# Moving preparation, gate closing, branch loads and the projection seam of a decoder-layer kernel

## The chip, the cores and the metric

The kernel runs on one core of one Trainium2 chip. The time is device microseconds of one execution, and the median over several executions is what counts.

## The reference

One layer of a hybrid decoder on 1024 tokens of width 1024, in float32. What is computed, cut to the main lines:

```python
h = rms_norm(x, norm1_g)
p_rwkv, p_sb, q_mem, gate_logits = split(h @ w_in)      # 1792, 1536, 512, 3072 columns
y_a = rwkv7_branch(p_rwkv, ...)       # 8 heads of 64: token shift, decay, delta-rule state, group norm
y_b = stick_breaking_branch(p_sb)     # 8 heads of 64, strictly causal
y_m = memory_branch(q_mem, mem, ...)  # 4 heads of 128 over 256 memory tokens
x = x + (sum_b sigmoid(gate_b) * (y_b @ w_branch[b])) @ w_out
h = rms_norm(x, norm2_g) @ w_up                          # 5632 columns
x = x + (silu(conv3(h)[gate]) * conv3(h)[value]) @ w_down
```

## The kernel before

Every matrix product is done with three matmuls on rounded operands: a number is split into a high part (an ACT copy to the type fp32r) and a low part (the difference, on DVE or POOL), and high·high, high·low and low·high are added in PSUM (`mm3`, L87). A projection of 128 columns over 1024 tokens takes eight steps of six matmuls, and the kernel treats one such step as the unit of interleaving.

The first half of the layer is written as Python generators that are woven together in `run`. A "main" stream (`rwkv_prep` for four pairs of heads, then `sb_attn`, `mem_attn`, `stage2` with the recurrent state, `group_norm`) takes a step, and a "pump" of projections (`items`: shifted projections of the recurrent branch, values, keys and queries, gates, memory projections, branch products) fills with a set number of steps for each (`weave`, L1631). The order in which an engine gets its instructions is then made by a planner that simulates the program with its own costs: it may move an instruction on its engine, except for those that are pinned (`pinned`, L108), each of which stays behind the instruction of its engine that the program gave just before it. All TensorE work from the recurrent preparation on is pinned. Most ACT, DVE and POOL work and all DMA issues are not. ACT, DVE and POOL then run their lists in order, and so does the queue of SP, which issues most loads.

Names that the change and the prediction touch:

- `shifted` (L241) takes a projection out of PSUM on DVE (L248), has ACT make the shifted copy (L249) and DVE join the two (L251). `shift_item` calls it after the eighth step.
- `rwkv_prep` has for each pair of heads two halves: `chain` makes the operands `bk` (L381) and `ra` (L382 to L384) on DVE, `decayed` (L410) scales `bk` on POOL, `gram` multiplies both on TensorE and masks the result on DVE (L398), `turned` transposes what `decayed` made. PSUM has four banks of tag `g` for these and four of tag `mm` for projections.
- `proj_item` is one projection of the pump; `gate_item` evicts one of gate logits (L739), multiplies with the row norm on DVE (L740), and leaves its sigmoid (L743) and its store (L745, on the ACT queue) to `close_gates`, which the next projection calls. The tile of the gate is one of three buffers of tag `w4`, which also serve keys, queries and squares.
- `norm_quarter` normalizes a quarter of the recurrent output in ten steps, laid between the twelve steps in which `stage2` makes the next quarter: sums, squares, the power -1/2 on POOL (`rsqrt`, L169), then four multiplications on DVE (L593).
- `load_y` loads four tiles of a branch's result (L1110) and rounds them (L1101 ACT, L1102 DVE) for `branch_item`. The loads go through `w4`; the low parts lie in four buffers of tag `A`, which the memory attention also uses; the high parts in one buffer `inst`.
- `out_proj` multiplies the merged branches with `w_out`, tile by tile of 128 tokens (`mm`). `norm` adds the residual (L1230), squares (L1231), takes the power on POOL, scales (L1235); `spread` transposes (two evictions per bank on ACT, two on DVE: L1250, L1252), `sums` (L1261 to L1266) and `split` (L1271, L1272) make the operands of the next stage.
- `up_phase` is a two-by-two block scheme of seven products instead of eight. `step(n, i)` is product i of column pair n, twelve matmuls. Its operands B11, B21, B22, T1 to T4 are what `split` makes. `hl` splits a weight (ACT L1351, POOL L1354).

Of the kernel before, what the change touches and what calls it, by code (L numbers as in the profile page):

```python
# [20 lines left out]
C = 64  # L21
# [6 lines left out]
OFF = 19.4  # L28
# [21 lines left out]
class Trunk:  # L50
# [120 lines left out]
    def startup(self):  # L171
# [41 lines left out]
        self.wa = self.shifted(12, "A", pps[0])  # L213
        nc.scalar.activation(self.wa[0:64], self.wa[0:64], AF.Tanh)
        self.sg = self.shifted(13, "A", pps[1])
        nc.scalar.activation(self.sg, self.sg, AF.Sigmoid)
        return self.shifted(4, "at", pps[2])
# [24 lines left out]
    def shifted(self, ti, tag, pp=None):  # L242
        nc = self.nc
        pp = pp or self.proj(self.I["w_in"][ti])
        pr, tmp = self.t4(), self.t4()
        nc.vector.memset(tmp[:, 0:1], 0.0)
        for h in range(2):
            nc.vector.tensor_tensor(pr[:, h * 512 : (h + 1) * 512], pp[h], self.nrb[:, h * 512 : (h + 1) * 512], ALU.mult)  # L248
        nc.scalar.activation(tmp[:, 1:1024], pr[:, 0:1023], AF.Copy, scale=self.mun[:, ti : ti + 1])  # L249
        out = self.t4(tag)  # L250
        nc.vector.scalar_tensor_tensor(out, pr, self.omm[:, ti : ti + 1], tmp, ALU.mult, ALU.add)  # L251
        return out
# [35 lines left out]
    def shift_item(self, ti, out, name):  # L288
# [10 lines left out]
        out.append(self.shifted(ti, "at", pp))  # L299
        self.fresh.append(name)  # L300
        yield
# [5 lines left out]
    def rwkv_prep(self, p, krv, need):  # L307
# [66 lines left out]
        def chain(h):  # L374
            hs = halves[h]
            bk, ra = self.t4("qk"), self.t4("qk")
            bk4, ra4 = (x.rearrange("p (c u s) -> p c u s", c=8, u=2) for x in (bk, ra))
            for x, first in ((b, 1), (kp, 0)):
# [3 lines left out]
            nc.vector.tensor_tensor(ra4[:, :, 0], self.c8(r[:, hs]), self.c8(P[:, hs]), ALU.mult)  # L382
            nc.vector.scalar_tensor_tensor(ra4[:, :, 1, 1:64], self.c8(P[:, hs])[:, :, 0:63], -1.0, self.c8(kk[:, hs])[:, :, 1:64], ALU.mult, ALU.mult)
            nc.vector.tensor_scalar(ra4[:, :, 1, 0], self.c8(kk[:, hs])[:, :, 0], -math.exp(OFF), None, ALU.mult)  # L384
# [188 lines left out]
    def norm_quarter(self, i, junk):  # L573
# [17 lines left out]
        yield  # L591
# [102 lines left out]
    def proj_item(self, src, fin, hook={}):  # L694
# [200 lines left out]
    def mem_kv(self):  # L895
# [18 lines left out]
        def ss():  # L914
            pst = self.ps("g")
            for j in range(2):
                for k in range(8):
                    o = (k % 4) * 256 + j * 128
                    self.colsum(pst[:, j : j + 1], sqs[k // 4][:, o : o + 128], self.ones[:, 0:1], k == 0, k == 7)
# [86 lines left out]
    def mem_q(self, h, out, hook):  # L1006
# [3 lines left out]
        def fin(pp):  # L1010
            sq = self.t4()
            qhi, qlo = self.t4("qk", F32R), self.t4("qk", F32R)
            for i in range(2):
                hs = slice(i * 512, (i + 1) * 512)
                nc.scalar.activation(qhi[:, hs], pp[i], AF.Copy, scale=self.par("memq"))
                nc.scalar.activation(sq[:, hs], pp[i], AF.Square)
                nc.vector.scalar_tensor_tensor(qlo[:, hs], pp[i], self.par("memq"), qhi[:, hs].bitcast(F32), ALU.mult, ALU.subtract)
# [127 lines left out]
    def branch(self, b, first):  # L1145
        st = {}

        def load():
            st["y"] = self.load_y(b)
# [6 lines left out]
        return load, items  # L1156
# [43 lines left out]
    def out_proj(self):  # L1200
# [21 lines left out]
        def norm(tt, pp):  # L1222
            x = self.t4()
# [4 lines left out]
            for n in range(2):  # L1228
                ns = slice(n * 512, (n + 1) * 512)
                nc.vector.tensor_tensor(x[:, ns], pp[n], x[:, ns], ALU.add)  # L1230
                nc.scalar.activation(sq[:, ns], x[:, ns], AF.Square, accum_out=ss[:, n : n + 1])  # L1231
            nc.scalar.dma_start(self.x2d[tt], x)
            nc.vector.tensor_tensor(rs, ss[:, 0:1], ss[:, 1:2], ALU.add)
            self.rsqrt(rs, rs, 1, 1.0 / D, 1e-6)
            nc.scalar.activation(sq, x, AF.Copy, scale=rs)  # L1235
            return sq

        def spread(tt, sq):
            tl = slice((tt % 4) * 128, (tt % 4 + 1) * 128)
            for kb in range(2):  # L1240
# [4 lines left out]
                for kk in range(4):  # L1245
# [3 lines left out]
                    if kk < 2:  # L1249
                        nc.scalar.activation(dst, src, AF.Copy, scale=self.par("g2", k))  # L1250
                    else:
                        nc.vector.tensor_scalar(dst, src, self.par("g2", k), None, ALU.mult)  # L1252
# [4 lines left out]
        def sums(t0, t1):  # L1257
            ts = slice(t0, t1)
            for j in range(2):
                b11, b21, b12, b22 = (x[:, :, ts] for x in halves(j))  # L1260
                nc.vector.tensor_tensor(b11, b12, b11, ALU.subtract)  # L1261
                nc.vector.tensor_tensor(t2[j][:, :, ts], b22, b11, ALU.subtract)
            for j in range(2):
                b11, b21, b12, b22 = (x[:, :, ts] for x in halves(j))
                nc.vector.tensor_tensor(b12, b22, b12, ALU.subtract)
                nc.vector.tensor_tensor(b21, t2[j][:, :, ts], b21, ALU.subtract)  # L1266

        def split(name, src, eng, ts=slice(0, 512)):
            for j in range(2):
                hi, lo = self.B[name][0][j][:, :, ts], self.B[name][1][j][:, :, ts]  # L1270
                nc.scalar.activation(hi, src[j][:, :, ts], AF.Copy)  # L1271
                self.pinned(eng.tensor_tensor(lo, src[j][:, :, ts], hi.bitcast(F32), ALU.subtract))  # L1272
# [3 lines left out]

        def late(tt):
            spread(tt, sqs.pop(tt))
            if tt == 3:
                for i in (0, 1):  # L1280
                    operand(("11", "21")[i], self.pool_l, "l4")
                    split(("11", "21")[i], [halves(j)[i] for j in range(2)], nc.gpsimd)
            elif tt == 5:
                sums(0, 256)
            elif tt > 5:
                sums(128 * tt - 512, 128 * tt - 384)
# [24 lines left out]
        w1 = weights(0, "at")  # L1311
        for tt in range(2):
            sqs[tt] = norm(tt, first[tt])
        for tt in range(2, 8):
# [5 lines left out]
            sqs[tt] = norm(tt, pp)  # L1320
        return [halves(j) for j in range(2)], t2, operand, split, late
# [4 lines left out]
    def up_phase(self, raws, t2, operand, split, late):  # L1326
        nc = self.nc
        old, new = slice(0, 384), slice(384, 512)
        operand("T2", self.pool_r, "T2", bufs=4)
        operand("T1", self.pool_l, "l4")  # L1330
        operand("T3", self.pool_r, "T3", bufs=4)
        operand("22", self.pool_r, "T22", bufs=4)
# [109 lines left out]

        def step(n, i):
            if i == 1:
                A = st[n, "A"] = bank()
                product(n, 1, A, True, True)
                p1 = st[n, "p1"] = self.r4("p1", n=512)
                nc.scalar.activation(p1, A, AF.Copy)  # L1448
# [52 lines left out]
        def parts(name, eng):  # L1501
            for ts in (old, new):
                split(name, src[name], eng, ts)

# [3 lines left out]
        split("T2", src["T2"], nc.vector, old)  # L1508
        split("22", src["22"], nc.gpsimd, old)
        step(0, 1)  # L1510
        step(1, 1)
        late(7)
        split("T2", src["T2"], nc.vector, new)
        split("22", src["22"], nc.gpsimd, new)
        load(1)
        prep2(0)
        parts("T1", nc.vector)
        step(0, 2)
        step(1, 2)
        prep3(0)  # L1520
        parts("T3", nc.vector)
        operand("T4", self.pool_a, "A", bufs=4)
        split("T4", src["T4"], nc.vector)
        st[0, 3] = hl(self.early[3][:, R], self.pool_l, ("l4", "l4"), 512, True)
        for i in (6, 5, 7, 4, 3):
            step(0, i)
            if i == 5:
                prep2(1)
            if i == 4:
                load(2)  # L1530
# [167 lines left out]
    def run(self):  # L1698
# [29 lines left out]
        for p in range(4):  # L1728
            kp, kss, qp, hooks = self.sb_qk(p, qk[p])
            items += [*([self.differ] if p == 0 else []), kp, gate(), *([self.spread_last] if p == 0 else []), kss, qp, gate(hooks), mark(f"sb{p}")]  # L1730
# [4 lines left out]
        items += [gate({0: prep}), gate(), gate({2: prep}), mss, *mv, *mk, mqi[0][0], mark("kv")]  # L1735
        items += [self.mem_kss, gate({1: mqi[0][1]}), self.mem_kbc, mqi[1][0], mark("mq0")]
        items += [mqi[2][0], mqi[3][0], gate({2: mqi[3][1], 4: mark("mq3")}), gate(), mark("mem")]
        ld1, br1 = self.branch(1, True)
        ld2, br2 = self.branch(2, False)
        items += [lambda: drain(inv), ld1, gate(), gate(), mark("y1"), *br1, ld2, gate(), *br2, gate()]  # L1740
# [114 lines left out]
```

## Time and profile before

| | |
|---|---|
| median of 3 runs | 1858.47 us (1855.64 to 1860.42) |
| profiled execution | 1856.43 us |
| its span, first to last instruction | 1854.7 us |
| TensorE busy | 1796.9 us, 97% |
| VectorE / ScalarE / GpSimd busy | 1170.1 / 866.7 / 788.6 us |
| mean granted TensorE clock | 0.991 |

In the profile PE is TensorE, DVE is VectorE, ACT is ScalarE, POOL is GpSimd, SP is the engine whose queue issues most loads. A row of the waits names who waited, at which line, for whom, the total, how often and the longest. A row of the timeline has the start, the time taken, the engine, the line and the tiles, and in brackets how long the engine had been idle and what ended it. A row of the stretches has a stretch, its length, and each engine's busy time, then the granted clock.

### The profile page before, as it was taken

Reading aid. Unit: us, or ns where it says so; the run is one execution under the profiler, and the core shown is the slowest. Engines: PE = TensorE matmul, PEld = TensorE weight load, DVE = VectorE, ACT = ScalarE, POOL = GpSimd, SP = SyncE. Lnnn points to the kernel's source line nnn. Section 1 sums busy time; section 2 is a strip of 40 time slices with the busy share of each in tenths; the row PEclk is TensorE's granted clock in tenths of the full one; section 3 lists DMA queues with packets and bytes.
Section 4 is the critical chain, followed back from the end, with each engine's and each line's share of the span. In section 5 each row is a group of like instructions: output and inputs, shape, how many; then the busy total and the mean of one; then the engine's idle time right before and its main releaser. Section 6 shows DMA issues by size and latency. Waiting matters only on the chain. (4 is left out here: it accounts for less than half of the span.)

```text
span 1854.7 us, 27269 instructions
## 1 busy us (share of the span) xinstructions
PE 1796.9 (97%) x10468; PEld 1451.4 (78%) x10468; DVE 1170.1 (63%) x1623; ACT 866.7 (47%) x1553; POOL 788.6 (43%) x447
## 2 busy tenths in 40 slices
PE   8999999999999999998999999979999999999999
PEld 6777778778787887776777878768888888878877
DVE  5657664998887514334333882467776777785595
ACT  5443343565565635533443443454454444444433
POOL 2322343222221452122322541487776767545454
PEclk9999999999999999999999999999999999999999
DMA  4155465111112441568654462323232233395475
GB/s 180 58 170 182 158 201 187 49 43 64 40 52 78 112 128 40 177 237 281 229 171 161 163 235 102 114 68 109 95 124 88 97 114 108 120 326 203 141 247 185
DMA packets 122339, 261.28 MB, mean 141 GB/s; under 512 B 28505, under 2 KB 43097, under 8 KB 122082
## 3 DMA queue, kind: packets, MB, share of 16 engines
q1 hardware_dynamic: 84738, 193.71, 32.2%
q10 hardware_dynamic: 33696, 53.23, 7.9%
q0 software_dynamic: 3776, 12.62, 2.2%
q8 instruction: 82, 1.34, 0.3%
q14 instruction: 47, 0.39, 0.1%
HBM read 178.99 MB, written 80.48 MB: 140 GB/s over the span
## 5 line engine op out<-in xcount | busy, mean ns | idle before, releaser
L81 POOL TENSOR_TENSOR wl<-wr,wh 128x1024 fp32r<-128x1024 f32 x77 | 195.0, 2533 | 479.8 <-ACT wh L80 479.8
L112 PE MATMUL mm<-xhi,wh 128*128 128x512 f32 x784 | 266.0, 420 | 9.1 <-ACT xhi L182 7.4
L112 PE MATMUL mm<-xlo,wh 128*128 128x512 f32 x784 | 247.2, 397 | 0.7 <-DVE xlo L183 0.7
L112 PE MATMUL mm<-xhi,wl 128*128 128x512 f32 x784 | 244.4, 393 | 0.0
L112 PEld LDWEIGHTS mm<-xlo,wh 128*128 128x128 f32 x784 | 149.5, 191 | 35.1 <-DVE xlo L183 1.5
L112 PEld LDWEIGHTS mm<-xhi,wl 128*128 128x128 f32 x784 | 148.9, 190 | 33.8 <-POOL wl L81 0.5
L112 PEld LDWEIGHTS mm<-xhi,wh 128*128 128x128 f32 x784 | 138.5, 192 | 39.8 <-issue 9.1
L80 ACT ACTIVATE wh<-wr 128x1024 fp32r<-128x1024 f32 x77 | 81.5, 1059 | 153.8 <-PE mm L112 89.6
L112 PE MATMUL mm<-dw,da 128*128 128x512 f32 x528 | 121.3, 390 | 1.5 <-DVE da L1593 1.4
L112 PE MATMUL mm<-BT,l 128*128 128x512 f32 x504 | 117.9, 389 | 1.0 <-POOL l L1354 1.0
L112 PEld LDWEIGHTS mm<-dw,da 128*128 128x128 f32 x528 | 98.9, 188 | 23.3 <-DVE da L1593 2.3
L1594 POOL TENSOR_TENSOR dw<-draw,dw 128x512 fp32r<-128x512 f32 x55 | 80.5, 1471 | 84.9 <-ACT dw L1592 82.2
L112 PE MATMUL mm<-BT,wh 128*128 128x512 f32 x352 | 109.8, 393 | 3.2 <-DVE u L1406 3.2
L838 DVE TENSOR_TENSOR_SCAN at<-at,nrt 128x128 f32<-128x128 f32 (+3 forms) x64 | 91.2, 1428 | 32.3 <-ACT at L832 32.2
L112 PEld LDWEIGHTS mm<-BT,l 128*128 128x128 f32 x504 | 94.5, 188 | 21.0 <-POOL l L1354 1.4
L112 PE MATMUL mm<-B,wh 128*128 128x512 f32 x352 | 108.5, 389 | 2.1 <-ACT p L1448 2.1
L1593 DVE TENSOR_TENSOR da<-draw,da 128x512 fp32r<-128x512 f32 x77 | 67.0, 878 | 60.3 <-ACT da L1591 59.7
L112 PE MATMUL g<-dw,da 128*128 128x512 f32 x396 | 92.4, 394 | 2.2 <-ACT dw L1592 1.1
L1354 POOL TENSOR_TENSOR l<-it,l 128x1024 fp32r<-128x1024 f32 x21 | 50.8, 2421 | 94.4 <-ACT l L1351 94.4
L112 PEld LDWEIGHTS g<-dw,da 128*128 128x128 f32 x396 | 75.4, 191 | 18.7 <-ACT dw L1592 1.6
L1591 ACT ACTIVATE da<-draw 128x512 fp32r<-128x512 f32 x77 | 48.3, 629 | 84.3 <-PE mm L112 41.0
L169 POOL TENSOR_TENSOR hf<-rs,half 128x16 f32<-128x16 f32 (+1 forms) x17 | 48.5, 2856 | 86.1 <-DVE rs L168 85.7
(329 smaller groups left out, 3982.2 us busy)
## 6 DMA issues: line engine op xcount, KB each, us to landing
wr<-in_w_in_dram SPq DMA_DIRECT2D x50, 512.0 KB, 3.6
draw<-actd SPq DMA_DIRECT2D x77, 256.0 KB, 3.4
draw<-in_w_down_dram SPq DMA_DIRECT2D x55, 256.0 KB, 4.6
at<-scr SPq DMA_DIRECT2D x24, 512.0 KB, 6.2
wr<-in_w_up_dram SPq DMA_DIRECT2D x22, 512.0 KB, 3.5
actd<-gall ACTq DMA_DIRECT2D x44, 256.0 KB, 3.3
rw<-in_w_up_dram SPq DMA_DIRECT2D x20, 512.0 KB, 3.9
gsd<-w ACTq DMA_DIRECT2D x18, 512.0 KB, 2.7
```

What stands on the lines that cost most here:

```text
L80: self.nc.scalar.activation(hi, raw, AF.Copy)
L81: self.nc.gpsimd.tensor_tensor(lo, raw, hi.bitcast(F32), ALU.subtract)
L112: self.pinned(self.nc.tensor.matmul(*a, **k))
L169: nc.gpsimd.tensor_tensor(out, t[:, :n], self.half[:, :n], ALU.pow)
L838: self.pinned(nc.vector.tensor_tensor_scan(sn[:, :W][:, ::-1], sn[:, :W][:, ::-1], self.nrt[:, 1152 - W :][:, ::-1], 1.0, ALU.mult, ALU.max))
L1354: nc.gpsimd.tensor_tensor(lo, src, hi.bitcast(F32), ALU.subtract)
L1591: self.pinned(nc.scalar.activation(A[:, 0], a, AF.Copy))
L1593: self.pinned(nc.vector.tensor_tensor(A[:, 1], a, A[:, 0].bitcast(F32), ALU.subtract))
L1594: nc.gpsimd.tensor_tensor(Wt[:, 1], w, Wt[:, 0].bitcast(F32), ALU.subtract)
```

## The change

It has seven parts.

1. Preparation: the last DVE instruction of a shifted projection (L251) comes one pump step later. `chain` makes `ra` before `bk`. The first `turned` of a pair, and the second `decayed`, come one step later.
2. `close_gates` is called after the fifth step of a projection instead of the third.
3. The power in `norm_quarter` is given two steps more before its result is used.
4. Memory part: the sums of squares of the memory tokens are made in two parts with a weight product between them, `spread_last` moves into a gate's seventh step, and the rounding of the memory queries is pinned.
5. Branch operands: the loads go straight into the buffers of the low parts, the high part is copied out, and the low part overwrites its own input. The eight instructions are pinned and given out one tile at a time in steps 4 to 7 of a gate projection. The first load moves behind one more gate.
6. Output projection: operand 11 is split after the fourth token tile as before, operand 21 only after the norm of the fifth. The norm of the last tile becomes three pieces, and its residual goes into a buffer of tag `l4`.
7. `up_phase`: the high and the low parts of the operands are written in a new order and pinned on ACT and DVE; the first eviction comes right behind its product; products 5 and 6 of the first pair change places; product 7 of the first pair gets a PSUM bank of its own instead of adding to that of product 6.

```diff
 def shifted(self, ti, tag, pp=None):
...
-        out = self.t4(tag)
-        nc.vector.scalar_tensor_tensor(out, pr, self.omm[:, ti : ti + 1], tmp, ALU.mult, ALU.add)
-        return out
+        def rest():
+            out = self.t4(tag)
+            nc.vector.scalar_tensor_tensor(out, pr, self.omm[:, ti : ti + 1], tmp, ALU.mult, ALU.add)
+            return out
+        return rest
...  shift_item
-        out.append(self.shifted(ti, "at", pp))
+        rest = self.shifted(ti, "at", pp)
+        yield
+        out.append(rest())
         self.fresh.append(name)
-        yield
...  rwkv_prep
         gram(0, 1, *u0)
         u1 = chain(1)
-        for _ in range(2):
+        for _ in range(3):
             yield
         turned(0, bp)
         bp = decayed(1, u1[0])
-        for _ in range(4):
+        for _ in range(3):
             yield
...  norm_quarter
         self.rsqrt(rs, vs, 16, 1.0 / 64, 64e-5)
-        yield
+        for _ in range(3):
+            yield
...  proj_item
-            if k == 2:
+            if k == 4:
                 self.close_gates()
...  load_y
-        ys = []
+        hi = self.pool_a.tile([128, 4, 1024], F32R, name=self.nm("yhi"), tag="inst")
+        los = [self.t4("A", F32R) for _ in range(4)]
         for k in range(4):
-            y = self.t4("w4")
-            self.nc.sync.dma_start(y, self.yd[b, k])
-            ys.append(y)
-        return self.split_y(ys)
+            self.nc.sync.dma_start(los[k].bitcast(F32), self.yd[b, k])
+        def part(k):
+            y = los[k].bitcast(F32)
+            self.pinned(self.nc.scalar.activation(hi[:, k], y, AF.Copy))
+            self.pinned(self.nc.vector.tensor_tensor(los[k], y, hi[:, k].bitcast(F32), ALU.subtract))
+        return [(hi[:, k], los[k]) for k in range(4)], [lambda k=k: part(k) for k in range(4)]
...  branch
+            hooks.update({3 + k: parts[k] for k in range(4)})
...  out_proj
-            x = self.t4()
+            x = self.t4() if tt < 7 else l4("x7", F32)
...
             if tt == 3:
-                for i in (0, 1):
-                    operand(("11", "21")[i], self.pool_l, "l4")
-                    split(("11", "21")[i], [halves(j)[i] for j in range(2)], nc.gpsimd)
+                side(0)
...
+            drain(norm(tt, pp))
+            if tt == 4:
+                side(1)
...  up_phase
+        hi("22", old)
+        hi("T1", old, (0,))
+        hi("T2", old)
+        next(norm)
+        lo("T1", old, (0,))
+        next(norm)
+        hi("T1", old, (1,))
+        lo("T2", old)
+        lo("22", old, eng=nc.gpsimd)
         step(0, 1)
-        step(1, 1)
-        late(7)
+        evacuate(0)
+        next(norm, None)
+        st[1, "A"] = bank()
+        product(1, 1, st[1, "A"], True, True)
+        spread()
+        evacuate(1)
+        sums(384, 512, (0,))
...
+        step(0, 5)
+        prep2(1)
+        step(0, 6)
+        Bk = bank()
+        product(0, 7, Bk, True, True)
+        v = st[0, "u2"] = u_tile()
+        nc.vector.tensor_tensor(v[:, L2], Bk, st[0, "u1"][:, R2], ALU.add)
...  run
-        items += [lambda: drain(inv), ld1, gate(), gate(), mark("y1"), *br1, ld2, gate(), *br2, gate()]
+        items += [lambda: drain(inv), gate(), ld1, gate(hk1), mark("y1"), *br1, ld2, gate(hk2), *br2, gate()]
```

More of the change, by code (lines that the diff above doesn't have):

```diff
@@ L1268, in split @@
-        def split(name, src, eng, ts=slice(0, 512)):
-            for j in range(2):
+            sub = lambda o, x, y: self.pinned(nc.vector.tensor_tensor(o, x, y, ALU.subtract))
+            for half in which:
+                for j in range(2):
+                    b11, b21, b12, b22 = (x[:, :, ts] for x in halves(j))
+                    if half == 0:
+                        sub(b11, b12, b11)
+                        sub(t2[j][:, :, ts], b22, b11)
+                    else:
+                        sub(b12, b22, b12)
+                        sub(b21, t2[j][:, :, ts], b21)
@@ L1311, in out_proj @@
         w1 = weights(0, "at")
+        drain = lambda g: [None for _ in g]
         for tt in range(2):
-            sqs[tt] = norm(tt, first[tt])
+            drain(norm(tt, first[tt]))
         for tt in range(2, 8):
```

146 lines of the change are left out of this document (81 added, 65 removed).

## The prediction

> **What bounds the kernel.** I read the page's busy shares first, then TensorE's waits stretch by stretch, then the granted clock around each wait, then the timeline of the engine that each wait names.
>
> ```profile
> span 1854.7 us, 27269 instructions
> PE 1796.9 (97%) x10468; PEld 1451.4 (78%) x10468; DVE 1170.1 (63%) x1623; ACT 866.7 (47%) x1553; POOL 788.6 (43%) x447
> ...
> PE g L105 <- DVE at L398: 6.4, 3, 2.6
> PE g L112 <- DVE qk L384: 2.3, 2, 1.7
> PE g L105 <- DVE at L251: 0.4, 1, 0.4
> ...
> PE g L105 <- ACT at L850: 3.7, 2, 2.8
> PE g L112 <- ACT at L1053: 2.8, 1, 2.8
> PE g L105 <- DVE at L838: 1.6, 1, 1.6
> PE mm L112 <- DVE qk L1017: 1.2, 1, 1.2
> ...
> PE mm L112 <- ACT w L739: 0.8, 1, 0.8
> ...
> PE g L112 <- ACT qk L549: 6.0, 1, 6.0
> PE g L112 <- ACT qk L561: 1.0, 1, 1.0
> ...
> PE mm L112 <- DVE u L1406: 3.2, 2, 2.5
> PE mm L112 <- ACT p L1448: 2.1, 1, 2.1
> PE g L105 <- ACT w L1235: 2.1, 1, 2.1
> PE mm L112 <- DVE u L1470: 1.6, 1, 1.6
> PE mm L112 <- POOL l L1354: 1.0, 1, 1.0
> PE mm L112 <- POOL wl L1354: 0.9, 1, 0.9
> PE mm L112 <- DVE BT L1272: 0.6, 1, 0.6
> ```
>
> The four blocks of waits are 50 to 320 us (preparation), 300 to 800 (both attentions), 850 to 1000 (recurrent state), 1160 to 1262 (seam between output projection and up projection). TensorE is the bound from end to end: it stands for 1854.7 - 1796.9 = 57.8 us. The change adds and removes no matmul, so all it can do is to remove or make waits of TensorE and change the clock at which it runs. The clock is the second half of the price:
>
> ```profile
> 100.00:108.00 8.00, 5.77 (x23) 4.69 (x22) 4.57 (x9) 3.13 (x4) 1.90 (x1) 0.79 0.58 205
> 150.00:158.00 8.00, 6.32 (x36) 4.53 (x37) 7.91 (x12) 2.21 (x2) 1.18 (x2) 0.80 0.71 257
> 494.00:500.00 6.00, 4.01 (x13) 3.34 (x14) 5.93 (x8) 3.30 (x6) 0.00 (x0) 0.72 0.37 150
> 867.00:879.00 12.00, 5.96 (x54) 4.82 (x53) 8.06 (x12) 4.38 (x15) 2.72 (x2) 0.72 0.87 301
> 984.00:992.00 8.00, 6.59 (x51) 4.79 (x52) 3.64 (x10) 1.76 (x8) 2.96 (x2) 0.79 0.17 68
> 1168.00:1176.00 8.00, 5.92 (x24) 4.55 (x23) 1.13 (x4) 2.29 (x5) 5.49 (x5) 0.79 0.47 133
> 1224.00:1232.00 8.00, 6.82 (x22) 5.14 (x23) 1.64 (x4) 2.64 (x3) 7.92 (x6) 0.79 0.02 3
> ```
>
> The column before the last two is the granted clock. 8 us at 0.79 lose 0.21 x 8 = 1.7 us of full clock, 6 us at 0.72 the same, 12 us at 0.72 lose 3.4. So a wait that pulls the clock down costs itself plus about 1.7 us, and waits as short as 1.0 us (984 to 992) were enough here.
>
> [...]
>
> **The change part by part.** For each the waits in question, the value taken, and both ends.
>
> *Preparation.* Waits 6.4 + 2.3 + 0.4 = 9.1 us, clock 1.7 + 1.6 = 3.3. Behind them stands DVE:
>
> ```profile
> DVE at L251 <- ACT w L249: 12.1, 10, 1.3
> ...
> 90.80 2.87 DVE L383 SCALAR_TENSOR_TENSOR qk<-qk,at 128x504 f32<-128x504 f32 x1
> ...
> 98.91 0.68 DVE L383 SCALAR_TENSOR_TENSOR qk<-qk,at 128x504 f32<-128x504 f32 x1
> ```
>
> DVE stands 1.2 us before each joining instruction L251, while ACT makes the copy, and the masks L398 that free PSUM are queued behind. One step later that copy is done, and the masks go ahead. The step is covered by six matmuls. With `ra` first, POOL's `decayed` starts behind all of `chain` and no longer beside it: L383 took 2.87 us beside a POOL instruction and 0.68 without. That POOL instruction is needed only by `turned`, which itself moves one step back, so the 1.9 us of it stay covered. Not all goes: the weight splits on POOL still fall beside DVE. Ends: 12.4 gained, or 3.8 lost if `turned` waits a full 1.9 us twice. Taken: 7.5, nearer to the first, since the cause is in the rows.
>
> *Gate closing.*
>
> ```profile
> 494.39 1.06 ACT L743 ACTIVATE w<-w 128x1024 f32<-128x1024 f32 x1 [4.99 <-DVE w L740]
> ...
> gsd<-w ACTq DMA_DIRECT2D x18, 512.0 KB, 2.7
> ```
>
> ACT stood 4.99 us before a sigmoid because DVE had not multiplied yet; the evictions L850 behind it came late, TensorE waited 2.8 us and lost 1.7 of clock. Two steps later DVE is done. What is delayed with it is the store, so the `w4` buffer comes free two steps later. Ends: 4.5 gained or 4.5 lost (the same stall met at a later evictor). Taken: 3.5.
>
> *Memory part and `spread_last`.* The waits for L1053 (2.8) and L1017 (1.2) may go or double; the sums in two parts hold a `g` bank during a weight product; pinning makes the query rounding wait its turn. No row says which. Ends: 4.0 either way. Taken: 0.
>
> *Branch operands.*
>
> ```profile
> 871.73 1.06 ACT L1101 ACTIVATE yhi<-w 128x1024 fp32r<-128x1024 f32 x1 [4.83 <-DMA w<-yd]
> ...
> w<-yd SPq DMA_DIRECT2D x8, 512.0 KB, 4.9
> ...
> 1161.89 5.60 PE L112 MATMUL mm<-qk,mg 128*128 128x512 f32 x24
> ```
>
> This is the largest wait: the planner put a rounding that waits for its load in front of five state evictions L549, ACT stood 4.83 us, TensorE 6.0. In the change the load needs an `A` buffer, free when the first branch's products are through, and the rounding stands four to seven steps into the gate behind them, at 6 matmuls each (24 of them take 5.60 us, so 1.4 a step) plus the state's own steps. Five to ten us for a load of 4.9 is enough. The loads also stand in SP's queue until the buffers are free, with the state's loads behind. Ends: 9.4 gained (6.0 + 3.4 of clock), 4.9 lost if one load is missed whole. Taken: 7.5, as some of the low clock lies inside the wait. The first branch's operands have no wait now and get none: its rounding lies under two gates.
>
> *Power in the norm.*
>
> ```profile
> DVE qk L593 <- POOL hf L169: 12.2, 4, 3.1
> ```
>
> DVE stands 3.1 us four times; once TensorE waits 1.0 and loses 1.7 of clock. The twelve steps of the new order fit the twelve of a quarter. Ends 0 and 2.7, taken 1.5.
>
> *Seam.*
>
> ```profile
> 1159.73 9.47 POOL L1272 TENSOR_TENSOR B<-raw,B 128x1024 fp32r<-128x1024 f32 x4 [6.38 <-ACT B L1271]
> 1169.16 0.54 POOL L169 TENSOR_TENSOR ss<-rs,half 128x1 f32<-128x1 f32 x1
> ...
> L1354 POOL TENSOR_TENSOR wl<-wsec,wh x1: 9842/9842/9842, 1216.0 to 1216.0; 128x1024 fp32r<-128x1024 f32 x1
> ...
> L1354 POOL TENSOR_TENSOR wl<-wr,wh x1: 2407/2407/2407, 1232.2 to 1232.2; 128x1024 fp32r<-128x1024 f32 x1
> ```
>
> The fifth tile's power waited behind four low parts on POOL. With two of them moved behind it POOL is free at about 1159.7 + 9.47/2 = 1164.5, and the wait of 2.1 for L1235 goes with its 1.7 of clock: taken 3.5 of 3.8. The eviction L1448 comes right behind its product: 2.1, with the 0.6 for L1272 2.7, taken 2.2. The rest is 3.2 + 0.9 + 1.0 + 1.6 = 6.7 and 1.7 of clock. The own bank of product 7 removes the wait for DVE; the low part of its weight, 9.84 us beside DVE's splits against 2.41 alone, is still POOL's. Ends 8.4 gained, 4.0 lost; taken 2.5, nearer to no change, as POOL's list is as long as before. If the cover of the last residual's load fails, the pinned evictions stand behind it.
>
> *Sum.* 7.5 + 3.5 + 0 + 7.5 + 1.5 + (3.5 + 2.2 + 2.5) = 28.2. Against it stands the new order of unpinned work: between 300 and 800 us, where little was aimed at, the rows above have 10.1 us of waits, with 1.7 of clock 11.8, or 2.4 per 100 us. About 350 us are planned anew, and I expect new waits there as dense as these: 8 off. Gain 20. The profiled execution took 1856.4 (its span and 1.7 around it), 2.0 under the median of 1858.5; in profile time I expect 1836.4, as a median 1838.5.
>
> **Rivals.**
>
> *POOL keeps the seam and takes more.* TensorE reaches product 7 earlier, while POOL's low part of the weight still runs beside DVE. For it: the 9.84. Against: the new order leaves DVE waiting for ACT more often, and POOL gets in there. Price: the 2.5 not gained, 4.0 lost, 1.7 of clock: gain 12, time 1846.5.
> [...]
>
> *The change does not do what it says.* The moved instructions of the preparation and the gates are unpinned, so the planner can put them where they were; and DVE is nearly full after it:
>
> ```profile
> 300.00:620.00 320.00, 311.48 (x2100) 253.55 (x2099) 263.25 (x255) 184.16 (x333) 81.73 (x36) 0.99 0.19 59
> ```
>
> 263 of 320 us. Then preparation and gates give 0, the branch loads meet the state's loads in SP's queue and give 3, the seam 5, and the 8 of new waits take it back: 1858.5.
>
> *Slower: the gate's buffer.* Three buffers `w4`; key and query projections need two at once. A gate closed two steps later must finish its sigmoid (1.06) and store (2.7), 3.8 us, in the three steps left, 4.2 us where nothing is woven in. Where ACT or the store is late by more than 0.4, the next eviction stands, and the evictions of attention behind it. Eight gates stand beside such projections; at 2.8 us each that is 22.4. With the rest as forecast (28.2 - 3.5 - 8 = 16.7): 1858.5 - 16.7 + 22.4 = 1864. Against it: among attention a step is longer.
>
> **How the numbers follow.** Forecast 0.56, its own range 1826 to 1850 (the seam's and the preparation's ends); POOL 0.15; no effect 0.13; slower 0.16. Faster by over 0.3% (5.6 us, about what a measurement of this kernel can tell from no change) holds for the first two: 0.71. Same 0.13, slower 0.16. The range is 1824, where nearly all the waits named go, to 1864, the slower case.
>
> **What would show it.** The wait for L549 and the low clock around 871 us gone, and no wait for a load in its place; DVE's waits before L251 gone, and those of TensorE for L398 under 2 us in all; no wait for L1235 in the fifth tile and for L1448; in the attention no new wait for the evictions of gates, keys and queries. TensorE's total of waits should fall from 57.8 to some 40. If it falls and the span doesn't, the clock is what I misjudged; if waits stand where none were, it is the planner's order.

## The result, and the profile after

The changed kernel takes 1837.8 us (median of 4 runs, 1836.9 to 1839.2) beside 1858.3 us for the kernel before (4 runs); the ratio is 0.9891, 95% interval 0.9874 to 0.9908. That is 20 us less, as forecast (1838.5), and inside the range. The profiled execution took 1837.9 us, its span is 1836.1.

The page's busy shares and then rows of TensorE's waits (waiting engine and line, releaser and its line: total, times, longest):

```profile
span 1836.1 us, 27283 instructions
PE 1790.2 (97%) x10468; PEld 1445.6 (79%) x10468; DVE 1174.8 (64%) x1622; ACT 865.7 (47%) x1553; POOL 784.1 (43%) x447
...
PE g L105 <- ACT at L856: 4.4, 2, 3.9
PE mm L112 <- POOL wl L81: 3.5, 2, 2.1
PE g L112 <- ACT qk L566: 2.2, 2, 1.4
PE g L105 <- DVE at L844: 2.1, 1, 2.1
PE g L112 <- DVE qk L389: 2.1, 2, 1.1
PE g L105 <- DVE at L403: 2.1, 1, 2.1
PE mm L112 <- DVE u L1506: 1.6, 1, 1.6
...
PE mm L112 <- POOL l L1384: 1.6, 1, 1.6
...
PE g L105 <- ACT w L1252: 0.6, 1, 0.6
```

TensorE now stands 1836.1 - 1790.2 = 45.9 us (57.8 before; some 40 were expected). Gone are the waits for the state's evictions (L549 before, 6.0), for the memory's exponentials (L1053 before, 2.8), for the up projection's first eviction (2.1) and most of that for the scaled copy (2.1, now 0.6). The masks L403 (L398 before) fell from 6.4 to 2.1. But the wait for L856 has grown from 3.7 to 4.4, that for L566 (L561 before) from 1.0 to 2.2, and the row for the weights' low parts L81 is new.

The same stretches as before the change, with the granted clock in the column before the last two:

```profile
100.00:108.00 8.00, 8.00 (x43) 6.47 (x43) 6.70 (x12) 3.18 (x4) 4.26 (x2) 1.00 0.86 301
150.00:158.00 8.00, 8.00 (x54) 6.44 (x51) 7.91 (x10) 1.06 (x1) 4.02 (x2) 1.00 0.67 242
494.00:500.00 6.00, 4.38 (x15) 3.52 (x16) 5.93 (x7) 3.26 (x6) 0.00 (x0) 0.72 0.21 87
867.00:879.00 12.00, 10.78 (x112) 8.01 (x112) 6.43 (x16) 6.54 (x19) 0.62 (x1) 1.00 0.85 304
984.00:992.00 8.00, 8.00 (x103) 6.32 (x101) 1.06 (x5) 4.75 (x15) 1.19 (x1) 1.00 0.41 145
1168.00:1176.00 8.00, 7.42 (x37) 5.97 (x36) 2.79 (x7) 3.11 (x9) 3.92 (x3) 1.00 0.14 56
1224.00:1232.00 8.00, 6.90 (x30) 5.03 (x28) 4.50 (x9) 2.58 (x4) 7.92 (x6) 1.00 0.16 57
```

Of these only 494 to 500, at the gates, is as low as before. Two others are low now: 258 to 266 us, at the first wait for L81 (0.79), and 340 to 348 (0.79, last section).

To see where the time went, I matched the 5960 projection matmuls of 512 columns (tiles `mm`) one to one, since the change leaves their order (but for products 5 and 6 of the first pair, which are of equal length), and subtracted start times. In the table below, worked out from the traces, a number says how much later than in the changed kernel the same matmul starts; the first row is the kernel before, the others are the experiments.

```
at (us, changed kernel)      329.9  346.3  534.8  661.6  743.0  886.0  989.0 1100.0 1179.2 1225.9 1518.9
kernel before                  3.2    1.1    0.4   -1.3    3.2   10.0    9.0    8.0   11.0   17.1   17.1
e1 three moves undone          1.8    0.2    0.2    0.2    0.2    0.2   -0.8    1.0    0.2    0.8    0.8
e2 branch undone               0.1    0.0    0.1    0.1    0.1    6.8    6.8    8.7    8.3    8.3    8.3
e3 seam undone                -0.4   -1.9   -3.5   -3.5   -3.5   -1.9   -1.9   -0.6    0.9    7.0    7.0
e4 gates pinned                0.0    0.0   -5.5   -7.6   -7.6   -7.6   -7.6   -6.6   -7.0   -5.7   -5.7
e5 query pins undone           1.9    0.3    0.4    0.4    3.6    3.6    3.6    2.1    2.1    2.4    2.3
e6 preparation undone          1.9    1.9    2.2    2.3    2.3    3.9    2.3    1.3    1.5    3.1    3.1
e7 turned undone               2.8    1.3    1.3    1.3    1.3    1.3    1.3    1.1    0.7    0.6    0.6
e8 norm pinned                -0.4   -0.5   -0.5   -0.4   -0.4    1.0   -3.5   -1.2   -0.9   -0.9   -0.9
e9 gates and norm pinned      -0.6   -2.2   -7.8   -9.8   -9.8  -10.3  -14.7  -14.2  -14.0  -11.2  -11.2
e10 e9, sums in one            1.3   -0.3   -5.8   -9.8   -9.7  -11.2  -15.7  -15.0  -15.2  -13.7  -13.4
e11 changed kernel again      -0.2   -0.2   -0.2   -0.2   -0.2    1.4   -0.2    1.6    2.1    2.0    2.0
e12 rounding unpinned         -0.2   -1.7   -0.8   -0.8   -1.3    4.1    2.6    5.1    5.0    6.9    6.9
```

By the first row the preparation brought 3.2 us by 330; 2.1 of them were given back at one wait at 342 us, which was 0.5 longer in the changed kernel, and at which this execution lost clock (0.79) and that of the kernel before did not (1.00; last section). Behind it the attention lost 2.4 (1.1 to -1.3), the memory part gained 4.5, the recurrent state 6.8 (by 886 us), and the seam 9.1 (8.0 at 1100 us to 17.1). The row of e11 says how far two executions of one kernel differ: up to 2.1. It moves by itself around 886 us and between 989 and 1100, so differences of other rows there are counted against it too.

### The profile page after: what moved, and what is told of

Same layout as the page of the kernel before. It is cut to its first block, busy times and chain, and to the rows that moved or that the text cites. A ratio compares the mean times of both kernels' runs of the same rounds, so it can differ in the third digit from the quotient of the medians.

```text
span 1836.1 us, 27283 instructions
## 1 busy us (share of the span) xinstructions
PE 1790.2 (97%) x10468; PEld 1445.6 (79%) x10468; DVE 1174.8 (64%) x1622; ACT 865.7 (47%) x1553; POOL 784.1 (43%) x447
## 4 chain that ended last, share of the span: by engine, by line
PE 66%; DVE 8%; issue 3%; POOL 2%; DMA 2%; ACT 2%; SPq 0%; ACTq 0%; DVEq 0%; POOLq 0%
PE mm L112 54%; PE g L112 9%; PE g L105 2%; DVE it L469 1%; DVE at L844 1%; DVE inst L471 1%; DVE qk L807 1%; DVE qk L790 1%; POOL dw L1655 1%; DVE mg L1213 1%; POOL wl L81 0%; DVE at L1206 0%; DMA at<-scr 0%; DVE qk L791 0%; DVE at L1205 0%
## 5 line engine op out<-in xcount | busy, mean ns | idle before, releaser
L81 POOL TENSOR_TENSOR wl<-wr,wh 128x1024 fp32r<-128x1024 f32 x77 | 194.7, 2530 | 509.1 <-ACT wh L80 500.7
L844 DVE TENSOR_TENSOR_SCAN at<-at,nrt 128x128 f32<-128x128 f32 (+3 forms) x64 | 87.5, 1371 | 39.4 <-ACT at L838 39.4
L746 DVE TENSOR_TENSOR w<-w,nrt 128x1024 f32<-128x1024 f32 x24 | 50.7, 2114 | 57.7 <-ACT w L745 54.6
```

The source lines that it names most:

```text
L81: self.nc.gpsimd.tensor_tensor(lo, raw, hi.bitcast(F32), ALU.subtract)
L746: nc.vector.tensor_tensor(g, g, self.nrb, ALU.mult)
L844: self.pinned(nc.vector.tensor_tensor_scan(sn[:, :W][:, ::-1], sn[:, :W][:, ::-1], self.nrt[:, 1152 - W :][:, ::-1], 1.0, ALU.mult, ALU.max))
```

## Experiments

The theory: each pinned or re-placed instruction acts at its own wait, and what is unpinned was put back by the planner and gives nothing. The rival, in several forms: the gain comes from the new order as a whole, so that parts don't add up. The edits are to the changed kernel. Four groups were run; the kernel before, run beside each, had medians of 1860.5 (e1 to e4), 1863.3 (e5 to e8), 1856.7 (e9 to e11) and 1860.0 us (e12). So times of different groups differ by some us for nothing, and I go by ratios and by the table for anything under 5 us. The changed kernel's own ratio was 0.9891 and 0.9897.

**e1: the three unpinned moves undone.**

```diff
-            if k == 4:
+            if k == 2:
                 self.close_gates()
...
-        for _ in range(3):
-            yield
+        yield
         for p, y in enumerate(ys):      # norm_quarter
...
-        rest = self.shifted(ti, "at", pp)
-        yield
-        out.append(rest())
+        out.append(self.shifted(ti, "at", pp)())
         self.fresh.append(name)
+        yield
```

> The changed kernel (1837.8 us) with its three moves of unpinned instructions taken back: the gates close at the third product again, one step stands ahead of the norm's multiplications, the joining instruction stands behind its copy again. Theory: the planner had put these moves back already, so they give nothing: 1837.8, between 1835.8 and 1839.8, and TensorE waits as before the taking back (the wait at 495 us near 3.9 us). Rival: they carry the 3.2 us that the preparation gained and some of the recurrent state's 6.8, because they free PSUM and DVE at the right moment: then 1841 to 1845, with TensorE's waits for the masks near 149, 203 and 213 us larger by 3 us in all.

1838.6 us, ratio 0.9879 (0.9857 to 0.9901): nothing. TensorE's list is the same, and of the 1622 DVE and 1553 ACT instructions in the trace fewer than ten stand elsewhere, among them a single sigmoid, which has changed places with one neighbour. In the changed kernel ACT still stood before a sigmoid, now 6.1 us (4.99 before); rows of ACT's timeline, and of ACT's and DVE's waits:

```profile
494.02 1.06 ACT L749 ACTIVATE w<-w 128x1024 f32<-128x1024 f32 x1 [6.06 <-DVE w L746]
```

```profile
ACT w L749 <- DVE w L746: 43.6, 21, 6.1
...
DVE qk L599 <- POOL hf L169: 12.2, 4, 3.1
DVE at L253 <- ACT w L249: 10.9, 9, 1.3
```

DVE's wait for the power is to the tenth what it was, and that for the shifted copy is 10.9 instead of 12.1. The planner had brought all three back.

**e4: the gates' sigmoid pinned.**

```diff
-                nc.scalar.activation(g, g, AF.Sigmoid, scale=-1.0)
+                self.pinned(nc.scalar.activation(g, g, AF.Sigmoid, scale=-1.0))
```

> The changed kernel with one thing added: each gate's sigmoid is kept behind the instruction that ACT was given just before it, so that the planner can't move it forward again and the gates do close two steps later. Theory: the wait of 3.9 us at 495 us and its low clock go (5.5 us less), other waits of the attention hardly change: 1832.3, between 1830 and 1836. Rival (the gate's buffer, the slower case of the prediction): the sigmoid and the store come too late for the next key and query evictions, which wait for a w4 buffer; then 1842 to 1860, with new waits of TensorE for evictions of ACT between 300 and 800 us.

1832.5 us, ratio 0.9857 (0.9835 to 0.9878). The wait of TensorE for L856 is gone altogether, there is no new wait for an eviction between 300 and 800 us, and the clock at 495 us is full (1.00). ACT's timeline, and the stretch in this kernel:

```profile
491.96 1.09 ACT L856 ACTIVATE at<-g 128x512 f32<-128x512 f32 x2
494.10 1.06 ACT L749 ACTIVATE w<-w 128x1024 f32<-128x1024 f32 x1 [1.05 <-DVE w L746]
```

```profile
490.00:500.00 10.00, 10.00 (x72) 8.35 (x71) 9.90 (x10) 4.70 (x11) 0.70 (x1) 1.00 0.30 107
```

The sigmoid runs at the same time as before; the evictions now stand in front of it and no longer behind. The table has 5.5 us there, and 2.1 more by 662, with two shorter waits gone from TensorE's list (0.9 for L691, 0.5 for L856). The slower rival of the prediction, the gate's buffer, was given its chance here and didn't come.

**e8: the norm's multiplications pinned.**

```diff
-            nc.vector.tensor_tensor(g3(y), g3(y), b3(rs, p), ALU.mult)
+            self.pinned(nc.vector.tensor_tensor(g3(y), g3(y), b3(rs, p), ALU.mult))
```

> The changed kernel with the norm's four multiplications kept behind the instruction that DVE was given just before, so that the planner leaves the steps ahead of them. Theory: DVE's four waits of 3.1 us for POOL's power go to under 2 us in all, and TensorE, which waits 0.8 to 1.4 us twice for L566 near 869 and 976 us, gains 0 to 2.7: taken 1.5, 1836.3. Rival: those waits of TensorE belong to ACT and its list, not to DVE: no change within 1 us, though DVE's waits go.

1835.3 us, ratio 0.9855 (0.9832 to 0.9878). One of DVE's four waits is left, TensorE's wait of 1.4 at 976 us is gone, and the clock from 972 to 990 us is 1.00 (0.91 in the changed kernel); DVE's and TensorE's waits in this kernel:

```profile
DVE qk L599 <- POOL hf L169: 3.1, 1, 3.1
```

```profile
PE g L112 <- ACT qk L566: 0.6, 1, 0.6
```

The table has 4.5 us there (1.0 to -3.5). Not all of it is the pin's: e11, the unaltered kernel, gains 1.6 at the same place (1.4 to -0.2): it has the same wait of 1.4, but a clock of 1.00 behind it. That leaves some 3. What is left at the end isn't settled: the trace says 0.9, or 2.9 against e11; the ratio is 3.6 permille lower, some 6.7 us, and its interval just meets that of the changed kernel.

**e2 and e12: the branch operands, undone, and with the new loads but unpinned rounding.**

```diff
 def load_y(self, b):                       # e2
+            y = self.t4("w4")
+            self.nc.sync.dma_start(y, self.yd[b, k])
...
-items += [lambda: drain(inv), gate(), ld1, gate(hk1), ...
+items += [lambda: drain(inv), ld1, gate(), gate(), ...
```

```diff
-            self.pinned(self.nc.scalar.activation(hi[:, k], y, AF.Copy))       # e12
+            self.nc.scalar.activation(hi[:, k], y, AF.Copy)
-            self.pinned(self.nc.vector.tensor_tensor(los[k], y, hi[:, k].bitcast(F32), ALU.subtract))
+            self.nc.vector.tensor_tensor(los[k], y, hi[:, k].bitcast(F32), ALU.subtract)
```

> The changed kernel with the branch operands as in the kernel before: loaded into w4 buffers ahead of the two gates, rounded by unpinned instructions. Theory: this edit alone removed the wait of 6.0 us at 872 us and its low clock, so the wait comes back there and the time rises by 6 to 9 us: 1844 to 1847. Rival: the wait had gone because the planner ordered the whole stretch anew (the memory part and the preparation moved too); then ACT's order at 872 us stays good without this edit, and the time stays within 2 us of 1837.8.

> The changed kernel with the new loads of the branch operands but without the two pins on their rounding, so that the planner places it again: in ACT's list three of the four roundings L1123 of the first branch move forward, to places ahead of the gate's eviction and of the state's evictions. Theory: the wait at 872 us came from where the rounding stands in ACT's list and not from the load's buffer; so it comes back, 4 to 7 us in all with its clock, 1842 to 1846, with ACT standing for the loads of yd there. Rival: loading into A buffers suffices, since the rounding is then planned by the late load; no wait for L554 near 872 us and 1837.8 within 2 us.

e2: 1843.9 us, ratio 0.9915 (0.9894 to 0.9936), some 4.5 us by the ratios; 6.7 us in the table, at the very place (5.1 against e11). TensorE's wait, ACT's row and the stretch in e2, then the stretch's answer in e12:

```profile
PE g L112 <- ACT qk L554: 5.5, 1, 5.5
```

```profile
868.15 1.06 ACT L1110 ACTIVATE yhi<-w 128x1024 fp32r<-128x1024 f32 x1 [4.31 <-DMA w<-yd]
```

```profile
860.00:885.00 25.00, 19.48 (x174) 14.80 (x173) 11.74 (x20) 10.48 (x30) 5.86 (x3) 0.86 0.72 259
```

```profile
860.00:885.00 25.00, 21.26 (x209) 16.33 (x209) 11.94 (x22) 11.58 (x36) 5.22 (x3) 0.86 0.68 251
```

In e12 the planner put three of the four roundings of the second branch in front of a group of the state's evictions L566 and the fourth between them (two stood in front in the changed kernel); TensorE waits 3.6 us for L566 in three pieces (0.8 in the changed kernel), the clock is 0.86 again, and the table has 5.4 us (-1.3 to 4.1), or 3.8 against e11. But it isn't the old wait: ACT stands only 1.6 us for the loads here (2.0 in the changed kernel). The low parts L1124, unpinned too, went between the state's multiplications L564 on DVE, and ACT's evictions L566 wait 4.4 us for those (2.2 in the changed kernel). So in this execution the places in the lists, DVE's as much as ACT's, bring back more than half of it, with the new load buffers kept. The time, 1842.2 us (ratio 0.9895, 0.9873 to 0.9917), can't tell e12 from the changed kernel, and the profiled execution was the slowest of six; what the buffers give alone stays open.

**e3: the seam undone** (the functions of the output projection's norm, spreading and sums and of the up projection's beginning as before; their diff stands above).

> The changed kernel with the functions of the output projection's norm, of its spreading and of the up projection's beginning as in the kernel before. Theory: the seam's edits act for themselves: the waits for the fifth tile's scaled copy (2.1), for the first eviction of the up projection (2.1) and for DVE's and POOL's parts (some 6) come back, and the time rises by the 10 us that the start times of equal matmuls showed between 1160 and 1250 us: 1848, between 1845 and 1851. Rival (POOL keeps the seam): part of those 10 us is the better clock of a core that comes to the seam with fewer waits behind it; then 1842 to 1845, and the low clock near 1172 and 1226 us stays away.

1848.4 us, ratio 0.9946 (0.9927 to 0.9966). The seam's waits are back, the largest to the tenth; waits of TensorE and then rows of POOL's timeline in e3:

```profile
PE mm L112 <- DVE u L1421: 3.2, 2, 2.5
PE mm L112 <- ACT p L1463: 2.1, 1, 2.1
...
PE g L105 <- ACT w L1250: 2.1, 1, 2.1
```

```profile
1151.14 9.46 POOL L1287 TENSOR_TENSOR B<-raw,B 128x1024 fp32r<-128x1024 f32 x4 [6.38 <-ACT B L1286]
1160.57 0.54 POOL L169 TENSOR_TENSOR ss<-rs,half 128x1 f32<-128x1 f32 x1
...
1205.85 9.84 POOL L1369 TENSOR_TENSOR wl<-wsec,wh 128x1024 fp32r<-128x1024 f32 x1 [2.09 <-ACT wh L1366]
```

The same rows of POOL in the changed kernel:

```profile
1151.76 4.77 POOL L1294 TENSOR_TENSOR B<-raw,B 128x1024 fp32r<-128x1024 f32 x2 [6.38 <-ACT B L1289]
1157.16 0.55 POOL L169 TENSOR_TENSOR ss<-rs,half 128x1 f32<-128x1 f32 x1 [0.63 <-DVE rs L168]
...
1201.62 2.44 POOL L1384 TENSOR_TENSOR wl<-wsec,wh 128x1024 fp32r<-128x1024 f32 x1 [3.17 <-ACT wh L1381]
```

The fifth tile's power comes behind two low parts instead of four. And the weight's low part, 9.84 us in e3 as in the kernel before, takes 2.44 us. DVE's low parts still run beside it, but now the long one is among them; DVE in the kernel before, then in the changed kernel:

```profile
1215.81 0.75 DVE L1272 TENSOR_TENSOR BT<-t,BT 128x256 fp32r<-128x256 f32 x2
```

```profile
1201.37 2.97 DVE L1294 TENSOR_TENSOR BT<-t,BT 128x256 fp32r<-128x256 f32 x2
```

The second of the two starts behind POOL's instruction at 1201.70 and ends behind it at 1204.34. So the price went from POOL to DVE and became smaller: one DVE instruction takes 2.6 us beside one of POOL, where before one of POOL took 9.84 beside a whole series of DVE's. No run took the neighbour alone away, so that one lengthens the other stays the author's inference, and why POOL's is the short one here is open. From 1100 us on, ahead of the seam's first wait, the table has 7.6 us for the seam (-0.6 to 7.0), 7.2 against e11. By the ratios it is 10; the profiled execution of e3 was the fastest of nine. Which of the seam's pieces gives how much was not taken apart.

**e5: the pins on the memory's query rounding undone.**

```diff
-                self.pinned(nc.scalar.activation(qhi[:, hs], pp[i], AF.Copy, scale=self.par("memq")))
+                nc.scalar.activation(qhi[:, hs], pp[i], AF.Copy, scale=self.par("memq"))
-                self.pinned(nc.vector.scalar_tensor_tensor(qlo[:, hs], ...))
+                nc.vector.scalar_tensor_tensor(qlo[:, hs], ...)
```

> The changed kernel with the two pins on the rounding of the memory's queries taken away (ACT's rounding and DVE's low part unpinned as before); the sums in two parts and the new place of spread_last stay. Without the pins the first head's exponentials L1062 stand behind the next queries' evictions in ACT's list again. Theory: the pins alone, in the prediction named only as a loss, removed the wait of 2.8 us at 718 us: it comes back with its low clock, 1842.3, between 1840 and 1844. Rival: the 3.5 us of the memory part come from the sums or from spread_last; then no wait at 718 us and 1837.8 within 2 us.

1840.8 us, ratio 0.9884 (0.9864 to 0.9904), not told apart by time. The trace does tell: the wait is back, and the table has 3.2 us at it. The other two moves of that part, the sums and `spread_last`, were not undone alone in the changed kernel. TensorE's wait and the stretch in e5:

```profile
PE g L112 <- ACT at L1062: 2.8, 1, 2.8
```

```profile
714.00:722.00 8.00, 5.11 (x32) 4.10 (x31) 2.77 (x9) 6.47 (x15) 3.15 (x2) 1.00 0.31 82
```

**e6 and e7: the preparation undone, and `turned` alone.**

```diff
-        for _ in range(3):
+        for _ in range(2):
             yield
         turned(0, bp)
         bp = decayed(1, u1[0])
-        for _ in range(3):
+        for _ in range(4):
             yield
...  e6 alone: bk ahead of ra in chain, joining instruction behind its copy
```

> The changed kernel with the whole preparation as before: bk ahead of ra, turned one step earlier, the joining instruction right behind its copy. Theory: the preparation is worth the 3.2 us that the start times of equal matmuls showed at 324 us, the later parts keep their gain: 1841.0, between 1839 and 1843; TensorE's waits for the masks are 6.4 us again. Rival: the better preparation only moves a wait into the attention, which starts with DVE later or earlier: then the gain is gone by 500 us and the time stays within 1 us of 1837.8.

> The changed kernel with turned alone one step earlier again; ra stays ahead of bk and the joining instruction stays delayed. Theory: DVE's list, which ra ahead of bk and not turned has changed, carries the gain (the masks come earlier), so this is worth less than half of the 3.2 us: 1838 to 1839.5. Rival: turned, pinned on TensorE, waits for POOL's decayed operand when it stands one step earlier, about 2 us twice or more: 1840 to 1843, with new waits of TensorE for POOL between 90 and 320 us.

e6: 1845.8 us, more than expected, though only some 3.3 us above the changed kernel by the ratio (0.9909, 0.9888 to 0.9929); the table has 1.9 us at the end of the preparation and 3.1 in all. e7: 1840.3 us, ratio 0.9881; the table has 2.8 at 330 us, and 1.5 of these come back at the wait at 342, where e7 kept its clock (1.00, last section). The rest, 1.3, is what its wait for the masks is longer.

TensorE's waits of the preparation in e6, then in e7:

```profile
PE g L105 <- DVE at L402: 6.4, 3, 2.6
PE g L112 <- DVE qk L388: 2.3, 2, 1.7
```

```profile
PE g L105 <- DVE at L403: 3.4, 1, 3.4
PE mm L112 <- POOL wl L81: 2.2, 1, 2.2
PE g L112 <- DVE qk L389: 2.1, 2, 1.1
```

With `turned` early the masks cost 3.4 instead of 2.1, still a wait for DVE and not for POOL's operand: e7's rival falls. What the changed order of `chain` does is mixed. It takes two mask waits away, but the row for L81 isn't in e6's preparation. It comes with the new order; in the changed kernel POOL's rows show why:

```profile
254.67 1.90 POOL L415 TENSOR_TENSOR it<-qk,pc 128x1024 f32<-128x1024 f32 x1 [8.72 <-DVE qk L389]
256.53 6.10 POOL L81 TENSOR_TENSOR wl<-wr,wh 128x1024 fp32r<-128x1024 f32 x2
```

POOL waits 8.72 us for `bk`, now the last of `chain`, and the two low parts behind it come late.

**e9, e10 and e11: both pins; with the sums of squares in one part as well; the changed kernel again.**

```diff
-lambda: mss(0), mv[0], lambda: mss(1), *mv[1:], *mk      # e10, beside the pins of e4 and e8
+lambda: (mss(0), mss(1)), *mv, *mk
```

> The changed kernel with both pins added: each gate's sigmoid and the norm's four multiplications kept behind the instruction given just before. Theory: the two act in different stretches (495 us and 980 us) and add up: the 5.5 of the gates and 1.5 to 3 of the norm come off, 1829 to 1831.5, at the side of the unaltered changed kernel in this same call. Rival: what one of them wins early is lost at the next fixed point, so the sum is no better than the gates alone: within 1 us of 1832.3.

> As the run with both pins, and the memory's sums of squares in one part behind each other again, as in the kernel before. Theory: the split is what made TensorE wait 1.4 us for POOL's low part of a weight at 659 us; in one part that wait goes and the time falls by 1.4 to 3 us below the run with both pins. Rival: the split is what keeps the memory's weights in time; undone, a wait as long or longer comes back between 640 and 740 us, and the time is the same or up to 3 us more.

> The changed kernel itself, unaltered, as the measure for the two other runs of this call. Both theories: 1837.8, between 1835 and 1841, as in its first run; its waits the same in place and size to 0.3 us.

e9: 1826.9 us (1824.6 to 1828.5), ratio 0.9830 (0.9804 to 0.9857). e10: 1824.1 us (1822.4 to 1828.3), ratio 0.9822 (0.9794 to 0.9849). e11: 1839.8 us; its waits are those of the first run to 0.3 us, but for two that are longer (2.0 instead of 0.9 for L1205, 1.1 instead of 0.6 for L1252). By the medians the two pins take 12.9 us off the changed kernel, run on the same chip; that is more than the 7 to 8.5 expected, and in the profiled execution 2.2 of it stand at 346 us, ahead of both pins, where the kernels don't differ (last section). In e9's row each gain stands at its own place: 5.6 between 346 and 535 us, as in e4, and 4.4 between 886 and 989, as in e8. So the pins add up. e10's further 2.8 is inside the spread of the runs. Its trace has the 1.4 us wait for L81 at 659 us gone, and 2.0 us gained between 535 and 662 as against e9. Either beats both kernels.

## Why the prediction was right, and where it wasn't

The time was right; its sum was right in part because misses cancelled. Term by term, in us, from the table, counted against the first execution of the changed kernel and against e11:

| step | taken | found | against e11 |
|---|---|---|---|
| preparation | 7.5 | 1.9 (e6) | 2.1 |
| gate closing | 3.5 | 0 (e1) | 0 |
| memory part | 0 | 3.2 (e5) | 3.2 |
| branch operands | 7.5 | 6.7 (e2) | 5.1 |
| power in the norm | 1.5 | 0 (e1) | 0 |
| seam | 8.2 | 7.6 (e3) | 7.2 |
| new waits | -8 | about -1 | about -1 |

The terms found come to 19.4 before new waits where the spans differ by 18.6, and to 17.6 against e11, whose span is 16.4 shorter than that of the kernel before. The last row is only this rest; no run measures it. Each term is a difference of single executions and good to 2 us.

*Branch operands* and *seam* went as written, through the waits named. The prediction had put the load's buffer first; e12, as far as one trace goes, brings back more than half of it without the pins. The rival "POOL keeps the seam" fell: POOL's 9.84 us became 2.44. That DVE's waits for ACT let POOL in, as the prediction had set against it, was not shown: POOL's instruction started at 1201.62 us, inside a run of DVE that had no wait from 1197.08 to 1213 us.

*Gate closing* and *norm power*: the mechanism was right, the step that failed is that the moves take place. The prediction had this among its rivals ("unpinned, so the planner can put them where they were"), for the whole kernel at 0.13. It should have been asked of each part: two parts are all unpinned, and for these it came true. e4 and e8 show that, once kept in place, they are worth 5.5 and some 3 to 4.5.

*Preparation*: the joining instruction was taken as the cause, and it did not move (10.9 of 12.1 us of DVE's waits are still there). The row of 2.87 us for L383 was also misread: beside it POOL ran a weight split L81 (90.29 to 93.13 us) and no longer `decayed` (88.43 to 90.33). Of the eight instructions L383, four took 2.4 to 2.9 us, all beside L81 and one of them beside `decayed` too; in the changed kernel (L384) three still do, two of them beside `decayed`. So the new order did not part the two. The rest of the gain came from `turned`, pinned on TensorE, and from `ra` first, and part of it went back into the new wait for L81. "The weight splits on POOL still fall beside DVE" was seen, their delay behind `decayed` wasn't.

*Memory part*: pinning was costed only as a loss for the query rounding. It put the rounding behind the first head's exponentials, which TensorE had waited for.

*New waits*: 8 us for 350 us planned anew was an extrapolation from the density of waits before. Two waits for L81 came (2.1 and 1.4), the longest wait for L856 grew by 1.1 and those for L566 by 1.2, and clock was lost (0.79 from 258 and from 340 us). Part of this lies inside the terms above; what is left beside them is about 1 us.

*The clock*: the prediction put about 1.7 us on top of a wait that pulls the clock down, and read from the stretches that waits of 1.0 us can be enough. In the changed kernel the stretch from 340 us lost clock at a wait of 2.1 (0.79 over 8 us, again 0.21 x 8 = 1.7); e3 had the same wait and kept its clock (1.00). So the size held; that every such wait pays it did not (last section).

## What to carry to other kernels

Where a planner orders the instructions, ask of every moved line whether it is kept there; compare the engines' lists before costing the move, and keep it in place if the wait is worth it. What an early instruction that waits costs is read from what stands behind it on its engine: in e2 a rounding on ACT stood 4.31 us for its load, and TensorE 5.5 us for the evictions behind it. A total that agrees doesn't prove its terms: undo the parts one at a time, and at this size read them from equal instructions' start times rather than from medians.

## What was not expected of the hardware

The same wait, of the same length (2.08 us), comes with a clock of 0.79 in one execution and of 1.00 in another. Row and stretch in the changed kernel:

```profile
342.54 0.33 PE L105 MATMUL g<-kon,at 128*128 128x128 f32 x1 [2.08 <-DVE at L844]
```

```profile
340.00:348.00 8.00, 5.92 (x22) 4.33 (x21) 7.93 (x9) 1.88 (x5) 1.42 (x1) 0.79 0.40 131
```

And in e3, where this part of the kernel is the same:

```profile
342.18 0.33 PE L105 MATMUL g<-kon,at 128*128 128x128 f32 x1 [2.08 <-DVE at L844]
```

```profile
340.00:348.00 8.00, 5.92 (x31) 4.49 (x31) 7.93 (x9) 2.66 (x6) 1.05 (x1) 1.00 0.40 131
```

Busy time is 5.92 in both, the clock 0.79 and 1.00. Thirteen of the traces have this wait of 2.1 us. In six (the changed kernel, e2, e4, e6, e8, e11) the stretch has a clock of 0.79 or 0.80, in seven 1.00, and in each of the seven TensorE gains 1.5 or 1.6 us between the first two columns of the table. The kernel before had a wait of 1.6 here and kept its clock, so this one wait makes the preparation look smaller by 346 us than it was at 330:

```profile
340.00:348.00 8.00, 6.44 (x31) 5.04 (x30) 7.93 (x8) 3.08 (x6) 4.83 (x3) 1.00 0.37 131
```

The wait of 2.8 at 718 us did the same: the clock was 1.00 in e5 (its stretch stands above), and 0.79 in the kernel before:

```profile
714.00:722.00 8.00, 5.23 (x25) 4.50 (x24) 4.08 (x11) 5.52 (x15) 3.15 (x2) 0.79 0.31 83
```

Why one execution lost clock and another did not was not shown: no run moved such a wait alone. For a forecast it means that the 1.7 us for the clock has about the right size (1.5 or 1.6 in the table), but is a chance for each wait, at this one six traces of thirteen, and not a fixed part of its price.
